# Moving the query and key projection of the last FoX pair into the stick-breaking stage

## The chip, the cores and the metric

The kernel runs on one core of a Trainium2 chip. The metric is the device time of one execution in microseconds (us). The profile is of one execution, with its engines called PE (TensorE's matmuls), PEld (its weight loads, which overlap the matmuls), DVE (VectorE), ACT (ScalarE), POOL (GpSimd) and SP (SyncE, which here only issues transfers).

## The reference, cut to what matters

One decoder layer over 2048 tokens of width 1024, in float32. The part that matters here is the token mixer: one input projection of the normed and modulated tokens `h`, and two groups of eight attention heads of 64.

```python
proj = h @ w_in[l]
q_f, k_f, v_f, q_s, k_s, v_s, f_logit = jnp.split(proj, offsets, axis=-1)
log_f = jax.nn.log_sigmoid(f_logit + b_fgate[l])
o_fox = forgetting_attention(q_f, k_f, v_f, log_f)   # softmax(q.k/8 + F[t] - F[s]), F = cumsum(log_f)
o_sb = stick_breaking_attention(q_s, k_s, v_s)       # sigmoid(z_ts) * prod_{s<j<t} (1 - sigmoid(z_tj))
mix = jnp.concatenate([head_rms_norm(o_fox), head_rms_norm(o_sb)], axis=-1)
x = x + gate_a * (mix @ w_out[l])
```

A gated MLP with a short convolution and a last norm follow.

## The kernel before

The tokens are cut into four blocks (`tb`) of 512, and each group's eight heads into four pairs (`p`) of two. A *unit* is one pair and one block: `units` lists them as stick-breaking (`sb`) pair 0, blocks 0 to 3, then pairs 1 to 3, then the same for `fox`, 32 in all. Attention is causal, so block 3 is the longest unit of a pair. A unit's attention (`attend`) makes logits on TensorE (`logits`, L378 and L379), works on them (stick-breaking: two sigmoids on ScalarE, a scan along the keys on VectorE, a product on GpSimd or VectorE; FoX: sum, minimum and exponential), and then goes through groups of two key blocks (`weighted`): four transposes (L388), a split of the result into a high and a low part by ScalarE and VectorE (L392, L393), and four matmuls with the values (L397). A pair has 72 such groups: 6, 14, 22 and 30 in its four blocks. At its end a unit stores its output (L509).

All products are of numbers split into a high and a low part, so each matrix product is three matmuls: high by high, high by low, low by high.

The projection of a unit runs ahead of its attention. `proj` loads the block of `h` as eight tiles from DRAM (L346; ten buffers), accumulates the queries (L281, 24 matmuls of 128x512) in one of two projection banks, and calls `finish_proj`. That splits the queries into `q2` (L289 on ScalarE, L290 on VectorE), spreads them over the two halves of the partitions into `Q` by four copies from SBUF to SBUF (L293), does the same with the keys (L281, 24 matmuls; L300, whose split is recorded at L44 and L45; copies into `K` at L303), and then makes the values. Values are made for two pairs at once by an even pair (L320, 96 matmuls of 128x256, spilled to DRAM for the other); an odd pair only loads them (L307). `Q` has two buffers, `K` five, `V` six, and the split tiles `q2` two. With block 0 of a pair, `load_w` loads and splits its weights (L256, L261).

`interleave` weaves the steps of the next unit's projection evenly between those of the current attention; in FoX a third generator, `late_mod`, prepares later weights, and the last unit carries the first part of the output projection (L629). The order in each engine's queue is then planned when the kernel is built, from the program's order and the buffers, and an instruction whose operands and buffers are there can be placed long before its place in the program. SP issues nearly all transfers, in order.

The pool `px` lies to the right in SBUF and holds four tiles `xt` of 4 KB per partition for the first stage's tokens. It is closed where FoX begins; the forget sums `Fb` (L672) and FoX's other tiles take its space.

Of the kernel before, what the change touches and what calls it, by code (L numbers as in the profile page):

```python
# [8 lines left out]
F32 = mybir.dt.float32  # L9
F32R = mybir.dt.float32r  # L10
# [6 lines left out]
P = 128  # L17
S = 2048
D = 1024
KT = D // P  # L20
HD = 64
NH = 8
NPAIR = 8
TB = 512
NTB = S // TB
# [8 lines left out]
def kernel(ctx: ExitStack, tc: tile.TileContext, x, c, w_ada, b_ada, g_attn, w_in, b_fgate,  # L34
                      g_out_fox, g_out_sb, w_out, g_mlp, w_up, conv_w, conv_b, w_down, g_final, out):
    nc = tc.nc
    x, out = x[0], out[0]
    w_ada, w_in, w_out, w_up, conv_w, w_down = w_ada[0], w_in[0], w_out[0], w_up[0], conv_w[0], w_down[0]

    def f(t):  # L40
        return t.bitcast(F32)

    def split(hi, lo, src, lo_engine=None):
        nc.scalar.activation(hi, src, AF.Copy)  # L44
        (lo_engine or nc.gpsimd).tensor_sub(lo, src, f(hi))  # L45

    const = ctx.enter_context(tc.tile_pool(name="const", bufs=1))
    dram = ctx.enter_context(tc.tile_pool(name="dram", bufs=1, space=DRAM))

    hs = [[dram.tile([P, 2, TB], F32, name=f"hs{t}_{k}") for k in range(KT)] for t in range(NTB)]  # L50
# [6 lines left out]
    vs = {k: [[dram.tile([P, 4, 2, P], F32, name=f"vs_{k}{p}_{t}") for t in range(NTB)] for p in range(2)]  # L57
          for k in ("sb", "fox")}
    zs = [dram.tile([4 * NH, P], F32, name=f"zs{t}") for t in range(NTB)]
    log_f = dram.tile([NTB * NH, TB], F32, name="log_f")  # L60
    fs = dram.tile([NH, S], F32, name="fs")
    rstd = [dram.tile([2 * NPAIR, TB], F32, name=f"rstd{t}") for t in range(NTB)]
# [68 lines left out]
    def interleave(main, n, fillers):  # L131
        live = [[g, k, 0] for g, k, _ in fillers if g is not None]
        for i, _ in enumerate(main):
            tick()
            for e in live:
                while e[2] < (i + 1) * e[1] / n:
                    e[2] += 1
                    if next(e[0], StopIteration) is StopIteration:
                        e[2] = 1 << 30
        for g, _, whole in fillers:  # L140
            if g is not None and whole:
                drain(g)
# [33 lines left out]
    def h_tile():  # L176
        return sl_.tile([P, 2, TB], F32R, name="hp", bufs=10)
# [101 lines left out]
    def accumulate(acc, n, w, h, kt):  # L279
        for i, (a, bb) in enumerate(((0, 0), (0, 1), (1, 0))):  # L280
            nc.tensor.matmul(acc, w[kt][:, a, n], h[:, bb], start=kt == 0 and i == 0, stop=kt == KT - 1 and i == 2)  # L281

    def finish_proj(kind, p, tb, aq, w, hts, res, ak=None):
        Q = sb.tile([P, 2, 2, TB], F32R, name="Q", bufs=2)
        K = sb.tile([P, 2, TB], F32R, name="K", bufs=5)
        V = sb.tile([P, 4, 2, P], F32R, name="V", bufs=6)
        q2 = sl_.tile([P, 2, TB], F32R, name="q2", bufs=2)
        k2 = sl_.tile([P, 2, TB], F32R, name="q2", bufs=2)
        nc.scalar.activation(q2[:, 0], aq, AF.Copy, scale=-HD ** -0.5)  # L289
        nc.vector.scalar_tensor_tensor(q2[:, 1], aq, -HD ** -0.5, f(q2[:, 0]), ALU.mult, ALU.subtract)  # L290
        for h in range(2):
            for r in range(2):
                nc.sync.dma_start(f(Q[r * HD:(r + 1) * HD, h]), f(q2[h * HD:(h + 1) * HD]))  # L293
        if ak is None:
            ak = pj()
            for kt in range(KT):
                accumulate(ak, 1, w[0], hts[kt], kt)
                if kt % 2:
                    yield
        split(k2[:, 0], k2[:, 1], ak, nc.vector)  # L300
        for h in range(2):
            for r in range(2):
                nc.sync.dma_start(f(K[r * HD:(r + 1) * HD, h]), f(k2[h * HD:(h + 1) * HD, r]))  # L303
        yield
        spill = vs[kind][p // 2][tb]
        if p % 2:
            nc.sync.dma_start(f(V), spill)  # L307
        else:
            V1 = sb.tile([P, 4, 2, P], F32R, name="V", bufs=6)
            forget = (kind, p) == ("sb", 0)  # L310
            step, width = (1, 2 * P + NH) if forget else (2, 2 * P)
            if forget:
                zn = px.tile([P, 4, NH], F32, name="zn", bufs=1)
            for i in range(0, 4, step):
                av = pj()
                for t in range(step):
                    tok = slice((i + t) * P, (i + t + 1) * P)
                    for kt in range(KT):
                        for m, (a, bb) in enumerate(((0, 0), (0, 1), (1, 0))):
                            nc.tensor.matmul(av[:, t * width:(t + 1) * width], hts[kt][:, a, tok],  # L320
                                             w[1][kt][:, bb, 0:width],
                                             start=kt == 0 and m == 0, stop=kt == KT - 1 and m == 2)
                        if kt % 4 == 3:
                            yield
                if forget:
                    nc.vector.tensor_copy(zn[:, i], av[:, 2 * P:width])
                av = av[:, 0:step * 2 * P].rearrange("p (t e h d) -> p t e h d", t=step, e=2, h=2)
                for e, v in enumerate((V, V1)):
                    v = v[:, i:i + step]
                    split(v[:, :, :, 0:HD], v[:, :, :, HD:P], av[:, :, e], nc.vector)  # L330
            if forget:
                b = pt()
                nc.tensor.transpose(b[0:4 * NH, 0:P], zn.rearrange("p t n -> p (t n)"), ident)
                zt = px.tile([4 * NH, P], F32, name="zt", bufs=1)
                nc.scalar.activation(zt, b[0:4 * NH, 0:P], AF.Identity, bias=bf_c)
                nc.sync.dma_start(zs[tb], zt)
            nc.sync.dma_start(spill, f(V1))
        res.append((Q, K, V))
        yield

    def proj(kind, p, tb, w, res):
        hts = []
        aq = pj()
        for kt in range(KT):
            h = h_tile()
            nc.sync.dma_start(f(h), hs[tb][kt])  # L346
            hts.append(h)
            accumulate(aq, 0, w[0], h, kt)
            if kt % 2:
                yield  # L350
        yield from finish_proj(kind, p, tb, aq, w, hts, res)

    def norm_proj(tb, xts, w, res):
        aq = pj()
# [170 lines left out]
    def late_mod():  # L525
# [47 lines left out]
        nc.vector.scalar_tensor_tensor(mod_m[:, 0], mod_m[:, 0], 1.0, cols[:, R_GM:R_GM + KT], ALU.add, ALU.mult)  # L573
        yield

    units = [(k, p, tb) for k in ("sb", "fox") for p in range(4) for tb in range(NTB)]
    weights = {}
    results = {}

    def proj_gen(u, xts=None):  # L580
        kind, p, tb = u
        if tb == 0:
            weights[kind, p] = load_w(kind, p)
            results[kind, p] = []
        if (kind, p) == ("sb", 0):
            return norm_proj(tb, xts or load_x(tb), weights[kind, p], results[kind, p])
        return proj(kind, p, tb, weights[kind, p], results[kind, p])
# [71 lines left out]
    for i, u in enumerate(units):  # L659
        kind, p, tb = u  # L660
        nxt = units[i + 1] if i + 1 < len(units) else None
        if u == ("sb", 1, 0):
            forget_sums()
        if u == ("fox", 0, 0):
            tick(1 << 20)
            close_pool("sx", "px")
            sx = open_pool("fx", side="right")
        if kind == "fox" and tb == 0:
            Fbs = [[sx.tile([P, TB], F32, name="Fb", bufs=8) for _ in range(NTB)] for _ in range(2)]
            for t in range(NTB):  # L670
                for h in range(2):
                    nc.sync.dma_start(Fbs[h][t],  # L672
                                      fs[2 * p + h:2 * p + h + 1, t * TB:(t + 1) * TB].to_broadcast([P, TB]))
        if kind == "fox":
            n = sum(2 * (2 + 2 * tb + j2 + 1) for j2 in range(2)) + 1
        else:
            n = sum(2 * (tb + 1 + 2 * tb + j2 + 1) for j2 in range(2)) + 1
        if i >= len(units) - 2:
            head_scale(i - len(units) + 2, pt(), sx)
        if nxt is None:  # L680
            drain(lm)
            close_pool("sl", "psa")
            psc = open_pool("psc", side="right", space=PSUM)
            p2a = open_pool("p2a")
            loaded = [load_o(0, p) for p in range(3)]
            wo = []
            tail = first_mix(loaded)
        steps = nxt and (KT + 11 if nxt[:2] == ("sb", 0) else KT - 1 if nxt[1] % 2 else KT + 4)
        interleave(attend(kind, p, tb, results[kind, p], Fbs), n,
                   [(nxt and proj_gen(nxt), steps, True),  # L690
                    (lm if kind == "fox" and (p, tb) != (0, 0) else None, 4, False), (tail, 12, True)])
    drain(first_out())
    tick(1 << 20)
# [327 lines left out]
```

## Time and profile before

| | |
|---|---|
| median of 3 runs | 3142.77 us (3141.69 to 3145.11) |
| the profiled execution | 3141.04 us, span 3139.3 us |
| TensorE matmul busy | 2967.0 us (95%) |
| TensorE weight loads busy | 2511.6 us (80%) |
| VectorE, ScalarE, GpSimd busy | 2145.5, 1691.0, 1227.1 us (68%, 54%, 39%) |
| stick-breaking attention from pair 1 on | 353.4 to 922.0 us of the span |
| FoX attention | 922.0 to 1602.1 us of the span |

The times of a stretch are counted from the start of the span. Busy time of an engine is the union of its instructions' records; since matmuls overlap in theirs, a busy TensorE need not be at its peak. The units' ends used below are the times at which SP issues the store of a unit's output.

### The profile page before, as it was taken

The page shows a single profiled execution, that of the slowest core. Times are in us where ns is not written, and L with a number is a line of the kernel's source. Part 1 is how long each engine was busy: PE and PEld are TensorE (multiplying, and loading weights), DVE is VectorE, ACT ScalarE, POOL GpSimd, SP SyncE. Part 2 cuts the span into 40 slices and gives each one's busy share as a digit, 9 for nine tenths or more (in the row PEclk, how much of TensorE's full clock was granted, in tenths as well). Part 3 has the DMA queues.
Part 4 walks back from the last instruction along what each step waited for, and adds up shares of the span by engine and source line. Part 5 has one row for each costly group of instructions (what it writes and reads, how often), then busy time and mean ns, then how long its engine had stood idle before and what let it go on. Part 6 is the DMA issues. An engine that isn't in the chain of part 4 may idle for free. (4 is left out here: it accounts for less than half of the span.)

```text
span 3139.3 us, 46425 instructions
## 1 busy us (share of the span) xinstructions
PE 2967.0 (95%) x15934; PEld 2511.6 (80%) x15934; DVE 2145.5 (68%) x3342; ACT 1691.0 (54%) x3161; POOL 1227.1 (39%) x1387
## 2 busy tenths in 40 slices
PE   6889998989989999999999999999899998999998
PEld 5778787877878889888877678888678887888887
DVE  6787888878875876556843587778987776354253
ACT  5666776666756676567744444444444444343332
POOL 1554455456553242242212344344444442322321
PEclk8999999999999999999999999999999999999999
DMA  9547542555336696585446632222222223554552
GB/s 267 177 140 255 168 136 69 182 185 155 123 108 221 214 314 211 158 313 162 164 158 222 212 97 86 86 83 83 82 82 89 85 81 130 190 199 161 189 199 90
DMA packets 292940, 496.51 MB, mean 158 GB/s; under 512 B 29448, under 2 KB 177664, under 8 KB 291680
## 3 DMA queue, kind: packets, MB, share of 16 engines
q1 hardware_dynamic: 281072, 480.92, 47.9%
q10 hardware_dynamic: 11632, 12.63, 1.1%
q8 instruction: 126, 2.06, 0.3%
q14 instruction: 110, 0.90, 0.1%
HBM read 352.61 MB, written 90.51 MB: 141 GB/s over the span
## 5 line engine op out<-in xcount | busy, mean ns | idle before, releaser
L810 PE MATMUL ps_o<-oa,wu 128*128 128x512 f32 x2088 | 503.5, 392 | 14.4 <-DVE oa L45 6.9
L810 PEld LDWEIGHTS ps_o<-oa,wu 128*128 128x128 f32 x2088 | 390.5, 188 | 105.5 <-DVE oa L45 10.7
L397 PE MATMUL ps_pv<-at,V 128*128 128x256 f32 x2304 | 410.9, 296 | 41.6 <-DVE at L393 24.8
L393 DVE TENSOR_TENSOR at<-ps_pt,at 128x512 fp32r<-128x512 f32 (+1 forms) x576 | 366.0, 653 | 102.8 <-ACT at L392 99.8
L281 PE MATMUL ps_pj<-hp,w_qk 128*128 128x512 f32 x1512 | 418.4, 406 | 11.1 <-ACT hp L44 3.1
L420 POOL TENSOR_TENSOR a<-a,r 128x512 f32<-128x512 f32 (+3 forms) x240 | 283.4, 1182 | 368.8 <-DVE r L416 112.3
L392 ACT ACTIVATE at<-ps_pt 128x512 fp32r<-128x512 f32 (+1 forms) x576 | 319.4, 577 | 179.8 <-PE ps_pt L388 147.3
L397 PEld LDWEIGHTS ps_pv<-at,V 128*128 128x128 f32 x2304 | 337.0, 192 | 84.6 <-DVE at L393 42.8
L281 PEld LDWEIGHTS ps_pj<-hp,w_qk 128*128 128x128 f32 x1512 | 275.7, 191 | 65.4 <-POOL hp L45 4.0
L45 DVE TENSOR_TENSOR wd<-wdraw,wd 128x1024 fp32r<-128x1024 f32 x88 | 112.4, 1277 | 261.4 <-ACT wd L44 261.4
L378 PE MATMUL ps_qk<-K,Q 128*128 128x512 f32 (+2 forms) x640 | 264.1, 414 | 11.3 <-DMA K<-q 5.8
L419 DVE TENSOR_TENSOR_SCAN r<-r 128x513 f32<-128x513 f32 x192 | 258.0, 1355 | 21.7 <-ACT r L410 14.5
L45 POOL TENSOR_TENSOR g<-graw,g 128x512 fp32r<-128x512 f32 x84 | 141.3, 1684 | 326.8 <-ACT g L44 326.8
L960 PE MATMUL ps_o<-wd,g 128*128 128x512 f32 x1040 | 250.8, 391 | 8.8 <-ACT g L44 8.8
L810 PE MATMUL ps_t<-ob,wu 128*128 128x512 f32 x984 | 243.2, 392 | 0.0
L320 PE MATMUL ps_pj<-w_v,hp 128*128 128x256 f32 (+1 forms) x1536 | 234.1, 291 | 4.8 <-DVE q L45 2.2
L379 PE MATMUL ps_qk<-K,Q 128*128 128x512 f32 (+2 forms) x640 | 238.1, 373 | 0.0
L960 PEld LDWEIGHTS ps_o<-wd,g 128*128 128x128 f32 x1040 | 196.2, 189 | 50.0 <-ACT g L44 9.2
L44 ACT ACTIVATE wu<-wuraw 128x512 fp32r<-128x512 f32 x214 | 133.2, 626 | 185.5 <-PE ps_o L810 111.5
L320 PEld LDWEIGHTS ps_pj<-w_v,hp 128*128 128x128 f32 x1536 | 211.8, 193 | 15.5 <-DVE q L45 3.1
L810 PEld LDWEIGHTS ps_t<-ob,wu 128*128 128x128 f32 x984 | 186.2, 189 | 39.4 <-DVE wu L45 0.3
L388 PE MATMUL ps_pt<-edge,a 128*128 128x128 f32 x1088 | 187.3, 281 | 27.6 <-POOL a L420 14.7
(217 smaller groups left out, 5743.3 us busy)
## 6 DMA issues: line engine op xcount, KB each, us to landing
hp<-hs SPq DMA_DIRECT2D x224, 512.0 KB
wuraw<-in_w_up_dram SPq DMA_DIRECT2D x84, 512.0 KB
wdraw<-in_w_down_dram SPq DMA_DIRECT2D x84, 512.0 KB
Q<-q SPq DMA_DIRECT2D x128, 256.0 KB
g<-u SPq DMA_DIRECT2D x42, 512.0 KB
graw<-g SPq DMA_DIRECT2D x84, 256.0 KB
hs<-hp SPq DMA_DIRECT2D x32, 512.0 KB
K<-q SPq DMA_DIRECT2D x128, 128.0 KB
```

The source lines that it names most:

```text
L45: (lo_engine or nc.gpsimd).tensor_sub(lo, src, f(hi))
L281: nc.tensor.matmul(acc, w[kt][:, a, n], h[:, bb], start=kt == 0 and i == 0, stop=kt == KT - 1 and i == 2)
L320: nc.tensor.matmul(av[:, t * width:(t + 1) * width], hts[kt][:, a, tok], w[1][kt][:, bb, 0:width], start=kt == 0 and m == 0, stop=kt == KT ...
L378: nc.tensor.matmul(b[:, :cw], Q[:, hl, 0, qcols], K[:, hl, :cw], start=True, stop=False)
L379: nc.tensor.matmul(b[:, :cw], Q[:, hl, 1, qcols], K[:, hl, :cw], start=False, stop=True)
L392: nc.scalar.activation(at[:, 0, lo:], b[:, lo:], AF.Copy)
L393: nc.vector.tensor_sub(at[:, 1, lo:], b[:, lo:], f(at[:, 0, lo:]))
L397: nc.tensor.matmul(o[:, 0:2 * P], V[kt // 4][:, kt % 4, hl, :], rhs, start=first and kk == 0 and w == 0, stop=last and kk == 1 and w == 1)
L419: nc.vector.tensor_tensor_scan(rev, rev, rev, 1.0, ALU.mult, ALU.bypass)
L420: (nc.vector if (ch + qi) % 4 == 0 else nc.gpsimd).tensor_mul(a[:, :need], a[:, :need], r[:, 1:need + 1])
L810: nc.tensor.matmul(b, w[:, p, j], o[:, q], start=first and i == 0, stop=last and i == 2, skip_group_check=True)
L960: nc.tensor.matmul(banks[t][n], g[:, a, t * P:(t + 1) * P], w[:, b, n * TB:(n + 1) * TB], start=k == 0 and i == 0, stop=k == NKD - 1 and i ...
```

## The change

The queries and keys of FoX pair 3 are no longer made in FoX. A new generator `far_proj(tb)` makes them for one block of tokens; it is appended to the next unit's projection in the last unit (block 3) of each stick-breaking pair, so that pair 0 makes block 0, pair 1 block 1 and so on. It accumulates queries and keys together in both projection banks over eight loads of `h`, splits them as before, and stores both split tiles in new DRAM tiles (`qks`). The first call loads and splits the weights once, and keeps them in the four buffers of `xt`. The number of filler steps of these four units grows by ten. In FoX, `stored_proj` replaces the projection of pair 3: it loads `Q` and `K` from DRAM in the same eight pieces, and the values as before, in one step.

```diff
+    qks = [[dram.tile([P, 2, TB], F32, name=f"{n}s{t}") for n in "qk"] for t in range(NTB)]
...
+    def spread_q(Q, q2):
         for h in range(2):
             for r in range(2):
-                nc.sync.dma_start(f(Q[r * HD:(r + 1) * HD, h]), f(q2[h * HD:(h + 1) * HD]))
+                nc.sync.dma_start(f(Q[r * HD:(r + 1) * HD, h]), q2[h * HD:(h + 1) * HD])
+
+    def spread_k(K, k2):
+        for h in range(2):
+            for r in range(2):
+                nc.sync.dma_start(f(K[r * HD:(r + 1) * HD, h]), k2[h * HD:(h + 1) * HD, r])
...
+    far = []
+
+    def far_proj(tb):
+
+        base = FAR * P
+        for kt in range(0 if far else KT):
+            raw = sl_.tile([P, 2, P], F32, name="raw_qk", tag="wraw", bufs=3)
+            nc.sync.dma_start(raw, w_in[kt * P:(kt + 1) * P, base:base + 5 * P].rearrange(
+                "p (a n) -> p a n", n=P)[:, 0:5:4, :])
+            if kt % 2 == 0:
+                two = px.tile([P, 2, 2, 2, P], F32R, name="w_far", tag="xt", bufs=4)
+            w = two[:, kt % 2]
+            split(w[:, 0], w[:, 1], raw)
+            far.append(w)
+        yield
+        aq, ak = pj(), pj()
+        for kt in range(KT):
+            h = h_tile()
+            nc.sync.dma_start(f(h), hs[tb][kt])
+            accumulate(aq, 0, far, h, kt)
+            accumulate(ak, 1, far, h, kt)
+            yield
+        q2 = qk_split(aq)
+        k2 = sl_.tile([P, 2, TB], F32R, name="q2", bufs=2)
+        split(k2[:, 0], k2[:, 1], ak, nc.vector)
+        for d, t in zip(qks[tb], (q2, k2)):
+            nc.sync.dma_start(d, f(t))
+        yield
+
+    def stored_proj(kind, p, tb, res):
+        Q, K, V = qkv_tiles()
+        spread_q(Q, qks[tb][0])
+        spread_k(K, qks[tb][1])
+        nc.sync.dma_start(f(V), vs[kind][p // 2][tb])
+        res.append((Q, K, V))
+        yield
...
     def proj_gen(u, xts=None):
         kind, p, tb = u
+        if (kind, p) == ("fox", FAR):
+            return stored_proj(kind, p, tb, results.setdefault((kind, p), []))
...
         steps = nxt and (KT + 11 if nxt[:2] == ("sb", 0) else KT - 1 if nxt[1] % 2 else KT + 4)
+        if nxt and nxt[:2] == ("fox", FAR):
+            steps = 1
+        ahead = nxt and proj_gen(nxt)
+        if (kind, tb) == ("sb", NTB - 1):
+            ahead, steps = chain(ahead, far_proj(p)), steps + KT + 2
         interleave(attend(kind, p, tb, results[kind, p], Fbs), n,
-                   [(nxt and proj_gen(nxt), steps, True),
+                   [(ahead, steps, True),
```

## Rows read from the trace of the kernel before

**Rows 1.** Windows by pair: length, busy (count) by engine, clock, DMA share, GB/s.
```profile
353.41:533.92 180.51, 162.75 (x1061) 142.24 (x1060) 160.45 (x220) 128.88 (x288) 94.22 (x145) 0.97 0.38 114
533.92:735.60 201.68, 188.79 (x1199) 165.87 (x1198) 162.68 (x222) 132.17 (x293) 96.66 (x153) 0.99 0.55 172
735.60:922.00 186.40, 166.06 (x1067) 144.76 (x1066) 155.18 (x200) 126.44 (x277) 110.92 (x150) 0.97 0.37 112
1278.38:1465.57 187.19, 184.62 (x1213) 166.30 (x1212) 112.33 (x285) 117.26 (x224) 66.71 (x81) 1.00 0.71 234
1465.57:1602.06 136.49, 130.40 (x847) 112.97 (x844) 104.25 (x271) 95.39 (x172) 24.06 (x43) 0.99 0.40 129
```

**Rows 2.** Windows, line L281 alone (query and key matmuls): PE busy, PEld busy.
```profile
353.41:533.92 180.51, 33.35 (x123) 21.95 (x123) 0.97 0.38 114
533.92:735.60 201.68, 67.66 (x256) 45.56 (x254) 0.99 0.55 172
735.60:922.00 186.40, 38.91 (x141) 24.95 (x141) 0.97 0.37 112
1339.94:1465.57 125.63, 50.08 (x192) 35.18 (x192) 1.00 0.79 269
...
1465.57:1602.06 136.49, 0.00 (x0) 0.00 (x0) 0.99 0.40 129
```

**Rows 3.** Window in the down-projection, columns as in the first group.
```profile
2669.00:2747.50 78.50, 78.50 (x348) 65.01 (x347) 23.69 (x18) 28.96 (x37) 31.19 (x19) 1.00 0.58 189
```

**Rows 4.** Windows: block 3 of stick-breaking pairs 0 to 3, FoX pair 2's blocks 2, 3.
```profile
250.53:353.41 102.88, 95.65 (x542) 79.86 (x541) 82.98 (x113) 68.51 (x141) 47.01 (x70) 1.00 0.71 241
462.67:533.92 71.25, 58.58 (x363) 49.16 (x362) 65.98 (x83) 49.88 (x110) 42.38 (x59) 0.95 0.28 89
653.37:735.60 82.23, 71.30 (x420) 59.61 (x419) 68.90 (x85) 53.87 (x116) 44.28 (x64) 0.98 0.46 148
850.70:922.00 71.30, 58.36 (x354) 49.23 (x353) 59.60 (x72) 45.30 (x94) 40.31 (x49) 0.95 0.28 86
1339.94:1465.57 125.63, 123.06 (x783) 109.55 (x782) 76.88 (x188) 82.36 (x149) 52.77 (x55) 1.00 0.79 269
```

**Rows 5.** Windows inside block 3 of stick-breaking pairs 1, 2 and 3.
```profile
472.00:520.00 48.00, 35.63 (x211) 28.29 (x209) 46.25 (x50) 35.26 (x75) 33.63 (x41) 0.93 0.20 54
680.00:712.00 32.00, 23.31 (x138) 18.25 (x139) 31.72 (x35) 22.62 (x46) 20.50 (x28) 0.96 0.09 20
864.00:904.00 40.00, 29.35 (x168) 23.74 (x168) 38.51 (x42) 28.33 (x57) 28.34 (x34) 0.91 0.11 34
```

**Rows 6.** The same windows, projection banks alone: PE, PEld, DVE, ACT.
```profile
472.00:520.00 48.00, 0.00 (x0) 0.00 (x0) 0.00 (x0) 0.65 (x2) 0.93 0.20 54
680.00:712.00 32.00, 0.00 (x0) 0.00 (x0) 0.66 (x1) 0.61 (x1) 0.96 0.09 20
864.00:904.00 40.00, 0.00 (x0) 0.00 (x0) 0.00 (x0) 0.00 (x0) 0.91 0.11 34
```

**Rows 7.** Timeline: start, length (us), instruction; a split, two groups of transfers.
```profile
455.94 0.69 DVE L45 TENSOR_TENSOR q<-ps_pj,q 128x512 fp32r<-128x512 f32 x1 [0.21 <-ACT q L44]
...
499.57 2.40 SPq L303 DMA_DIRECT2D K<-q  x4
...
926.04 4.83 SPq L672 DMA_DIRECT2D Fb<-fs  x8
```

**Rows 8.** Windows, line L629 in pair 3, line L320 in pair 2.
```profile
1465.57:1602.06 136.49, 24.95 (x96) 17.22 (x96) 0.99 0.40 129
...
1339.94:1465.57 125.63, 7.45 (x49) 6.52 (x47) 1.00 0.79 269
```

**Rows 9.** Groups by line and form: lines L290, L45 (count, ns minimum/median/maximum).
```profile
L290 DVE SCALAR_TENSOR_TENSOR q<-ps_pj,q x32: 660/684/693, 61.3 to 1452.2; 128x512 fp32r<-128x512 f32 x32
...
L45 DVE TENSOR_TENSOR q<-ps_pj,q x27: 664/691/693, 293.6 to 1473.5; 128x512 fp32r<-128x512 f32 x27
L45 POOL TENSOR_TENSOR w_qk<-raw_qk,w_qk x32: 727/741/1056, 730.7 to 1329.7; 128x256 fp32r<-128x256 f32 x32
```

**Rows 10.** Windows, line L281 alone, block 3 of stick-breaking pairs 0 and 1.
```profile
250.53:353.41 102.88, 53.59 (x201) 36.30 (x201) 1.00 0.71 241
462.67:533.92 71.25, 8.96 (x35) 6.30 (x36) 0.95 0.28 89
```

More of the change, by code (lines that the diff above doesn't have):

```diff
@@ L281, in accumulate, with qkv_tiles, qk_split, finish_proj @@
             nc.tensor.matmul(acc, w[kt][:, a, n], h[:, bb], start=kt == 0 and i == 0, stop=kt == KT - 1 and i == 2)
[L283 to L286, printed above, removed]
+    def qkv_tiles():
+        return (sb.tile([P, 2, 2, TB], F32R, name="Q", bufs=2), sb.tile([P, 2, TB], F32R, name="K", bufs=5),
+                sb.tile([P, 4, 2, P], F32R, name="V", bufs=6))
+    def qk_split(aq):
         q2 = sl_.tile([P, 2, TB], F32R, name="q2", bufs=2)
-        k2 = sl_.tile([P, 2, TB], F32R, name="q2", bufs=2)
         nc.scalar.activation(q2[:, 0], aq, AF.Copy, scale=-HD ** -0.5)
         nc.vector.scalar_tensor_tensor(q2[:, 1], aq, -HD ** -0.5, f(q2[:, 0]), ALU.mult, ALU.subtract)
+        return q2
+    def spread_q(Q, q2):
         for h in range(2):
             for r in range(2):
-                nc.sync.dma_start(f(Q[r * HD:(r + 1) * HD, h]), f(q2[h * HD:(h + 1) * HD]))
+                nc.sync.dma_start(f(Q[r * HD:(r + 1) * HD, h]), q2[h * HD:(h + 1) * HD])
[3 more added lines that the diff above has]
+                nc.sync.dma_start(f(K[r * HD:(r + 1) * HD, h]), k2[h * HD:(h + 1) * HD, r])
+    def finish_proj(kind, p, tb, aq, w, hts, res, ak=None):
+        Q, K, V = qkv_tiles()
+        q2 = qk_split(aq)
+        k2 = sl_.tile([P, 2, TB], F32R, name="q2", bufs=2)
+        spread_q(Q, f(q2))
         if ak is None:
@@ L300, in finish_proj @@
         split(k2[:, 0], k2[:, 1], ak, nc.vector)
-        for h in range(2):
-            for r in range(2):
-                nc.sync.dma_start(f(K[r * HD:(r + 1) * HD, h]), f(k2[h * HD:(h + 1) * HD, r]))
+        spread_k(K, f(k2))
         yield
@@ L351, in proj @@
         yield from finish_proj(kind, p, tb, aq, w, hts, res)
+    far = []
[18 more added lines that the diff above has]
+            yield
+        q2 = qk_split(aq)
+        k2 = sl_.tile([P, 2, TB], F32R, name="q2", bufs=2)
+        split(k2[:, 0], k2[:, 1], ak, nc.vector)
[3 more added lines that the diff above has]
+    def stored_proj(kind, p, tb, res):
+        Q, K, V = qkv_tiles()
+        spread_q(Q, qks[tb][0])
[3 more added lines that the diff above has]
+        yield
     def norm_proj(tb, xts, w, res):
@@ L574, in late_mod, with chain @@
         yield
+    def chain(*gens):
+        for g in gens:
+            yield from g
     units = [(k, p, tb) for k in ("sb", "fox") for p in range(4) for tb in range(NTB)]
@@ L578 @@
     results = {}
+    FAR = 3
     def proj_gen(u, xts=None):
         kind, p, tb = u
+        if (kind, p) == ("fox", FAR):
+            return stored_proj(kind, p, tb, results.setdefault((kind, p), []))
         if tb == 0:
```

## Prediction

> **What bounds the kernel now.** I read four views in this order. The busy time of each stretch comes first, cut at the ends of pairs: stick-breaking pairs 1 to 3 and FoX pairs 2 and 3 [rows 1, 2]. TensorE is busy for 81% to 99% of every one, so the page alone says "TensorE bound" everywhere. But matmuls overlap in their records, so busy is not full: the counts have to be priced.
>
> The price comes from a stretch of the down-projection in which TensorE does nothing but 128x512 matmuls without a gap: 78.50 us for 348, so 0.2256 us each [rows 3]. A block's queries and keys take 2 x 8 x 3 = 48 such matmuls, 10.83 us, and the four blocks of the last FoX pair 43.3 us.
>
> Where do those 192 matmuls stand? The stretch from 1339.94 to 1465.57 (attention of FoX pair 2, blocks 2 and 3) holds exactly 192 of the projection's matmuls [rows 2], and pair 3's own stretch holds none. So the planned order runs ahead of the program, and the work that the change takes away lies wholly in those 125.63 us. There TensorE is busy 123.06 us, VectorE 76.88 and ScalarE 82.36 [rows 4]: this stretch is TensorE's.
>
> The third view is the last block of each stick-breaking pair (four units) [rows 4]. TensorE's idle there is 7.2, 12.7, 10.9 and 12.9 us, 43.8 in all. The fourth cuts three of these units finer: for 48, 32 and 40 us in a row no projection matmul runs at all, VectorE is busy 96% to 99%, and TensorE 73% to 74% at a granted clock of 0.91 to 0.96 [rows 5, 6]. Why is there no filler? The next pair's projections have run up against their buffers: the keys of block 1 of pair 2 are split at 455.94 and are copied to their five-buffer tile only at 499.57, 43 us later [rows 7]. The new work needs none of those buffers. These holes are VectorE's time, and what TensorE does in them besides may be cheap.
>
> **The change, part by part.** *Removed from FoX.* 192 matmuls go, 43.3 us at the dense price: that is the most that the stretch can lose, and leaves 82.3 us. How fast can attention go with nothing else in TensorE's queue? Pair 3's stretch shows that: 136.49 us for its 72 weighted-sum steps (groups of two key blocks), among them 96 output-projection matmuls of the same shape [rows 1, 8], 21.7 us. So (136.49 - 21.7) / 72 = 1.594 us a step. Blocks 2 and 3 have 22 + 30 = 52 steps, 82.9 us; 49 value matmuls of half the width remain [rows 8], at half the price 5.5 us (an estimate). Together 88.4, so a gain of 37.2 us. If the output projection hid under pair 3's other work, the pace is 136.49 / 72 = 1.896, 98.6 us, and the gain 27.0. I take 37, between 27 and 43. VectorE keeps 71 us of work there and ScalarE under 82, so neither takes over below 88. The splits of four blocks go too; they were not the bound there.
>
> *Added to stick-breaking.* The same 48 matmuls for each of four blocks, plus per block two ScalarE copies and two VectorE splits of 0.684 and 0.691 us (median), 1.375 together [rows 9]. From below: matmuls in a hole cost nothing where VectorE sets the pace, but VectorE's own 1.375 us counts in full; four blocks, 5.5 us. From above: the pairs themselves, which differ mainly in how many projection matmuls they carry. Pair 2 has 133 more than pair 1 and takes 21.2 us longer, 0.71 of the 30.0 us at the dense price; against pair 3 it has 115 more and takes 15.3 longer, 0.59 of 25.9 [rows 1, 2]. At 0.71 a block costs 7.6 us, four 30.7. The last unit of pair 0 against that of pair 1 is worse still: 166 more matmuls, 31.6 us longer, 0.845 of 37.4 [rows 4, 10]; at that price four blocks cost 36.6.
>
> These slopes mix in other work (weight splits on VectorE in pair 0's unit, different values), and they are paid mostly where TensorE is already full. The new work has the hole beside it: 120 us of holes at about a quarter idle, some 32 us by the busy rows, for three blocks of 32.5 us. So I take 3.6 us for pairs 1 to 3, nearer to the hole than to the slope, and for pair 0, whose last unit already carries 201 such matmuls, the mean slope of 0.65, 7.0 us. Sum 17.8, call it 18; ends 5.5 and 36.6.
>
> *Room by another count.* Matmul records give 43.8 us of idle for 43.3 us of work, a tight fit, by which I would take the slope of 0.71 and forecast about 3137. The weight loads of the same rows leave 23.0, 22.1, 22.6 and 22.1 us uncovered, 89.8 in all [rows 4], by which the work fits twice and the price lies nearer the hole's. [...]
>
> *Weights.* The eight raw loads and splits move from FoX to the end of pair 0. GpSimd's eight splits take 8 x 0.741 = 5.9 us [rows 9]; in that unit it is busy 47 of 103 us [rows 4], so they hide, and they come well before a use. If that cover is gone, 5.9 us once. The split weights sit in the four old x tiles, which are idle by then: nothing.
>
> *Transfers.* Each block brings eight 512 KB loads and two 512 KB stores on SP's queue; the FoX side loses the eight loads, and reads its queries and keys in the same eight copies, now from DRAM. Transfers share 9% to 20% in the holes [rows 5], so bandwidth is free. A store waits for the split, and behind it in SP's queue stand the next projection's loads; who waits for them is the next pair's projection, which is 43 us ahead of its buffer [rows 7]. Nothing, or a few us if that lead is used up. The two small query/key buffers and both projection banks are held a block longer, against the same lead.
>
> *Start of FoX.* The tiles of the forget sums take over space in which the new weights lay. They are loaded at 926.04 [rows 7], 4 us after the last stick-breaking block is stored, and the last hole ends at 904, so the fourth block should be done. If it is late, FoX starts late by as much.
>
> *Sum.* The profiled execution took 3141.04 us, 1.7 below the median of the runs. 3141.0 - 37 + 18 = 3122; on the median 3123.8. I predict **3124 us**; by the nearer ends of both terms, 3111 to 3135.
>
> **The rivals.** *Slower.* The planned order puts filler matmuls ahead of attention's transposes and logits in TensorE's queue, which runs in order, and VectorE, which must not wait in the holes, waits. Place: the four last units; price 0.845 of dense, 36.6 us. With FoX giving 27, the result is 3152. It decides once stick-breaking costs more than FoX gives: at 37, that is 0.85 of 43.3. For it: the unit of pair 0. Against it: in pairs 1 to 3 the slope is 0.59 to 0.71 even without holes singled out.
>
> *No change.* TensorE's work is the same in total, and if its queue is the bound everywhere, moving is worth nothing: 30.7 back for 27 to 37 gained, 3137 to 3147. For it: busy shares of 81% and more. Against it: 120 us with no filler at a reduced clock.
>
> *Almost all of it.* The holes take the work at VectorE's 5.5 us and FoX falls to TensorE's bare remainder, 43: 3105. For it: the weight-load rows. Against it: FoX's pace without filler, and pair 0, which has no hole.
>
> **How the numbers follow.** Forecast 0.56, almost all of it 0.15, no change 0.12, slower 0.17. A change of 0.2%, 6.3 us, is about what a measurement of this kernel can tell from none. So faster 0.71, same 0.12, slower 0.17. The range of 3105 to 3147 holds the forecast, the no-change case, half of the larger gain and the mild end of the slower one.
>
> **What would show it.** FoX pair 2's blocks 2 and 3, 125.63 us now, should fall to 82 to 99 with no 128x512 projection matmul for pair 3 in them; pair 3's stretch should stay near 136 us. In stick-breaking the holes should carry 48 matmuls each with VectorE still over 90% busy; pairs 1 to 3 should grow by about 4 us each, and pair 0's last unit by 7. The prediction is wrong if VectorE's busy share in the holes falls below about 85%, if the next pair's projections come late to attention, or if FoX stays at its length because VectorE or ScalarE, not TensorE, holds it.

## The result, and the profile after

The changed kernel took 3148.38 us (median of 10 runs, 3143.89 to 3152.46), the kernel before 3141.19 beside it (10 runs): a ratio of 1.0022 [1.0012, 1.0032]. The forecast was 3124, its range ended at 3147. Timed once more, in another session (below), the change came out at 1.0001 [0.9992, 1.0010]. So it is worth nothing, or costs about 0.2%. (The ratios here and below come with their 95% intervals; they are taken over all the runs and differ by up to 0.0008 from the quotients of the medians.) The profiled execution took 3144.33 us (span 3142.5), against 3141.04 (3139.3) before.

The times at which SP issues the stores of the units' outputs say where the time went (us of the span; differences are of the unrounded times; the first unit's end, which no edit touches, varies by 2 us between runs). The last column is the fastest version found, told below as e14; it has a second edit besides, the square on ScalarE.

| end of | before | after | | blocks 2 and 3 alone | |
|---|---|---|---|---|---|
| stick-breaking pair 0, block 3 | 353.4 | 362.5 | +9.1 | 352.5 | -0.9 |
| pair 1, block 0 | 367.5 | 383.5 | +16.1 | 367.6 | +0.2 |
| pair 1, block 3 | 533.9 | 555.9 | +22.0 | 533.7 | -0.2 |
| pair 2, block 3 | 735.6 | 758.6 | +23.0 | 739.1 | +3.5 |
| pair 3, block 3 | 922.0 | 950.6 | +28.6 | 931.5 | +9.5 |
| FoX pair 2, block 1 | 1339.9 | 1368.3 | +28.4 | 1349.9 | +9.9 |
| FoX pair 2, block 3 | 1465.6 | 1468.2 | +2.6 | 1461.3 | -4.3 |
| FoX pair 3, block 3 | 1602.1 | 1601.8 | -0.2 | 1594.9 | -7.2 |
| the kernel | 3139.3 | 3142.5 | +3.3 | 3137.5 | -1.8 |

Stick-breaking pays 28.6 us and FoX gives back 28.8. What is left, 3.5 us, stands after attention, in the output projection and the MLP, which no edit touches. From attention's end to the last instruction the profiled execution of before took 1537.2 us, that of after 1540.7. A second profile of after took 1543.9 there, and the version in the last column 1542.6. This part scatters from execution to execution, and so do the stages before it. Four later runs (e1, e7, e12 and e13, told below) have the change's stick-breaking, and their edits, where they have one, touch FoX alone. With the profile above that makes five, in which stick-breaking ends 26.1 to 33.7 us later than before. In two runs with the stick-breaking of before (e2 and e8) it ends at 922.4 and 917.0. So a difference of under about 5 us between two single profiles decides nothing. Steadier in the five is where the growth stands: pair 0 ends 7.9 to 11.7 us later, pair 1 takes 12.6 to 13.1 us more, pair 2 changes by -0.9 to 1.0, and pair 3 takes 4.7 to 11.7 more.

The windows of the changed kernel that answer to [rows 1, 4] (length, then busy time and count of PE, PEld, DVE, ACT, POOL, the granted clock, DMA share, GB/s): three pairs, the four last units, then the two FoX stretches.

```profile
362.50:555.90 193.40, 176.43 (x1136) 154.00 (x1135) 171.64 (x230) 135.64 (x301) 105.08 (x150) 0.98 0.43 136
555.90:758.60 202.70, 195.78 (x1229) 173.63 (x1228) 161.39 (x223) 131.61 (x291) 89.42 (x148) 0.98 0.59 190
758.60:950.60 192.00, 174.76 (x1134) 152.69 (x1133) 160.62 (x204) 128.48 (x283) 111.63 (x155) 1.00 0.47 144
256.35:362.50 106.15, 100.33 (x558) 85.36 (x557) 74.84 (x106) 64.50 (x134) 41.97 (x64) 0.98 0.82 276
480.40:555.90 75.50, 61.91 (x388) 52.07 (x387) 69.87 (x85) 51.56 (x111) 45.61 (x61) 0.95 0.27 88
675.90:758.60 82.70, 78.20 (x450) 67.26 (x449) 68.19 (x86) 53.65 (x115) 37.08 (x59) 0.96 0.54 180
875.50:950.60 75.10, 61.01 (x399) 51.94 (x399) 63.56 (x76) 46.59 (x97) 44.05 (x52) 1.00 0.26 83
1368.30:1468.20 99.90, 86.06 (x608) 77.66 (x606) 78.55 (x184) 78.52 (x143) 52.50 (x56) 0.93 0.55 173
1468.20:1601.80 133.60, 128.10 (x845) 111.36 (x843) 104.35 (x270) 95.46 (x172) 24.07 (x44) 1.00 0.39 128
```

The pairs grew by 12.9, 1.0 and 5.6 us. Pair 2's last unit, 82.23 before, is 82.70 now with TensorE busy 78.20 instead of 71.30: there the idle time was used. Pair 1's and pair 3's last units grew by 4.3 and 3.8 us, and TensorE still idles 13.6 and 14.1 us in them, more than before (12.7 and 12.9 [rows 4]). FoX's stretch fell from 125.63 us to 99.90, and TensorE, which was idle 2.6 us in it, is now idle 13.8.

Where did the moved matmuls go? The next fence is of windows of the changed kernel, the tile of the new weights alone (PE, PEld, ACT, POOL): one window for each block's 48.

```profile
273.80:291.40 17.60, 12.24 (x48) 8.50 (x48) 0.00 (x0) 0.00 (x0) 1.00 0.92 280
420.50:442.30 21.80, 12.80 (x48) 8.58 (x48) 0.00 (x0) 0.00 (x0) 1.00 0.90 333
659.10:677.30 18.20, 11.97 (x48) 8.52 (x47) 0.00 (x0) 0.00 (x0) 1.00 0.93 298
819.90:841.10 21.20, 12.96 (x48) 8.54 (x48) 0.00 (x0) 0.00 (x0) 1.00 0.93 346
```

None stands in a hole (a stretch in which no projection matmul runs). Block 1's run ends at 442, block 3's at 841, while the last units that were to carry them begin at 480 and 875. The holes are still there, later. Windows of before and then of after, the projection banks alone (PE, PEld, DVE, ACT), each just inside the longest stretch of its pair in which no projection matmul starts:

```profile
468.80:520.90 52.10, 0.00 (x0) 0.00 (x0) 1.04 (x3) 1.08 (x3) 0.93 0.25 74
674.70:713.40 38.70, 0.00 (x0) 0.09 (x1) 0.66 (x1) 0.61 (x1) 0.96 0.21 62
856.80:909.20 52.40, 0.00 (x0) 0.00 (x0) 1.14 (x3) 1.09 (x3) 0.93 0.31 98
```

```profile
490.60:542.90 52.30, 0.00 (x0) 0.00 (x0) 1.03 (x3) 0.87 (x3) 0.93 0.28 85
718.70:738.30 19.60, 0.00 (x0) 0.06 (x1) 0.68 (x1) 0.59 (x1) 0.83 0.34 106
892.90:937.70 44.80, 0.00 (x0) 0.00 (x0) 1.14 (x3) 1.04 (x3) 1.00 0.36 114
```

Pair 1's hole is as long as it was, pair 3's lost 7.6 us, and only pair 2's was halved. The new matmuls went ahead of the holes, into stretches that were already full, and only in pair 2 did they push much of other work into one. The next fence has windows of before around the places where blocks 1, 2 and 3 went: TensorE is busy for 114.29 of their 115 us, at a granted clock of 1.00. Block 2's place was as full as the others'.

```profile
410.00:450.00 40.00, 40.00 (x270) 36.30 (x269) 32.18 (x45) 28.09 (x58) 20.54 (x35) 1.00 0.27 94
640.00:675.00 35.00, 35.00 (x208) 30.54 (x207) 22.17 (x32) 18.80 (x41) 12.26 (x21) 1.00 0.79 255
800.00:840.00 40.00, 39.29 (x266) 35.27 (x265) 34.01 (x45) 29.56 (x63) 21.50 (x32) 1.00 0.22 73
```

In FoX the stretch has a new bound. Windows of 20 us of the changed kernel, columns as in the first fence:

```profile
1368.30:1388.30 20.00, 18.68 (x140) 17.12 (x138) 12.99 (x35) 15.01 (x29) 13.21 (x13) 1.00 0.75 258
1388.30:1408.30 20.00, 8.19 (x43) 5.58 (x42) 14.97 (x19) 17.01 (x30) 18.68 (x17) 0.77 0.94 300
1408.30:1428.30 20.00, 19.96 (x137) 18.64 (x136) 16.87 (x43) 15.87 (x29) 14.85 (x15) 0.89 0.02 9
```

In the second of them TensorE works 8.19 of 20 us, GpSimd 18.68 and ScalarE 17.01. The timeline of the changed kernel there (start, length, instruction, count, idle before and releaser) shows GpSimd, VectorE and TensorE:

```profile
1398.38 8.60 POOL L602 TENSOR_TENSOR hp<-hp 128x512 f32<-128x512 f32 x7
...
1399.02 7.98 DVE L540 SCALAR_TENSOR_TENSOR ls<-ls 128x4 f32<-128x4 f32 x1 [3.67 <-ACT p L502]
1406.92 1.28 DVE L443 TENSOR_TENSOR at<-ps_pt,at 128x512 fp32r<-128x512 f32 x2
...
1407.66 1.76 PE L438 MATMUL ps_pt<-edge,p 128*128 128x128 f32 x7 [11.19 <-DVE at L443]
```

GpSimd makes additions of `late_mod` (L602: sums of weight rows that ScalarE has scaled at L601). VectorE's square of a 128x4 tile (L540, median 0.165 us) begins in the middle of seven of them and ends with them, 7.98 us later. TensorE waits 11.19 us. `late_mod`'s work is not new (28 such additions in the stretch, before and after), but it stands closer: between 1376 and 1420, 25 of these additions instead of 13. The next fence has L602 alone in after, then the same line, there L552, in before.

```profile
1376.00:1420.00 44.00, 30.28 (x25) 0.84 0.67 221
```

```profile
1376.00:1420.00 44.00, 16.25 (x13) 1.00 0.91 313
```

### The profile page after: what moved, and what is told of

It is laid out like the page before. It is cut to its first block, busy times and chain, and to the rows that moved or that the text cites. A ratio compares the mean times of both kernels' runs of the same rounds, so it can differ in the third digit from the quotient of the medians.

```text
span 3142.5 us, 46429 instructions
## 1 busy us (share of the span) xinstructions
PE 2968.5 (94%) x15934; PEld 2521.2 (80%) x15934; DVE 2160.1 (69%) x3342; ACT 1689.1 (54%) x3161; POOL 1226.8 (39%) x1387
## 5 line engine op out<-in xcount | busy, mean ns | idle before, releaser
L282 PE MATMUL ps_pj<-hp,w_qk 128*128 128x512 f32 x1320 | 367.6, 409 | 10.7 <-DMA hp<-hs 4.0
L45 DVE TENSOR_TENSOR wd<-wdraw,wd 128x1024 fp32r<-128x1024 f32 x88 | 113.4, 1290 | 260.6 <-ACT wd L44 260.6
L282 PEld LDWEIGHTS ps_pj<-hp,w_qk 128*128 128x128 f32 x1320 | 243.5, 193 | 58.7 <-DMA hp<-hs 5.1
L45 POOL TENSOR_TENSOR g<-graw,g 128x512 fp32r<-128x512 f32 x84 | 141.3, 1683 | 326.9 <-ACT g L44 326.9
L460 ACT ACTIVATE r<-ps_qk 128x512 f32<-128x512 f32 (+2 forms) x320 | 173.2, 541 | 69.7 <-PE ps_qk L429 63.3
```

## The experiments

Two questions: why do four blocks cost stick-breaking 28.6 us, and what holds FoX's stretch at 100? Two theories for the second: the wait of the square, or the burst of `late_mod` as such.

**The square on ScalarE (e1), and the same edit in the kernel before (e2).**

```diff
-                    nc.vector.scalar_tensor_tensor(l, l, EPS, l, ALU.mult, ALU.mult)
+                    nc.scalar.activation(l, l, AF.Square, scale=EPS ** 0.5)
```

> The changed kernel, with the square of FoX's sums (two small operands, both in SBUF) made by ScalarE and no longer by VectorE. In the changed kernel one such square lasts 7.98 us while GpSimd runs seven additions of 128x512 back to back, and TensorE is idle for 11.2 us right behind it. Theory (VectorE waits for GpSimd at their common way into SBUF): the wait goes, attention of FoX pair 2 blocks 2 and 3 takes 88 to 92 us and not 99.9, and the time falls by 8 to 11 us, to about 3138. Rival (the stretch is as long as its other work makes it, the wait only shows where slack lies): 98 to 100 us, and 3146 to 3149.

> Control: the kernel before with the same square on ScalarE. Before, no such square lasted over 1.3 us, so by both theories the time stays within 0.1% of before, 3138 to 3144.

Measured: e1 3143.30 us against 3148.31, 0.9992 [0.9983, 1.0002]; e2 3143.61, 0.9989 [0.9978, 1.0001]. No square of e1 is long any more, and its FoX stretch is 98.1 us instead of 99.9. Windows of e1, the whole stretch and 20 us of it, columns as above:

```profile
1366.80:1464.90 98.10, 89.54 (x610) 77.94 (x609) 70.48 (x179) 78.76 (x148) 52.68 (x56) 0.97 0.58 179
...
1387.10:1407.10 20.00, 15.53 (x82) 12.33 (x82) 11.74 (x30) 18.39 (x34) 20.00 (x19) 0.83 0.97 318
```

The rival's 98 to 100 us came out. With the wait gone GpSimd is busy 20.00 of 20 us and ScalarE 18.39: the wait fell into time that was lost anyway. Between e1 and e2, both with the edit, the change is worth nothing.

**The burst spread (e7), and the control (e8).** e1 and e2 with seven steps of `late_mod` in a unit instead of four, so that it ends before FoX pair 2's block 2.

```diff
-                    (lm if kind == "fox" and (p, tb) != (0, 0) else None, 4, False), (tail, 12, True)])
+                    (lm if kind == "fox" and (p, tb) != (0, 0) else None, 7, False), (tail, 12, True)])
```

> The changed kernel with the square on ScalarE and with seven steps of the late modulation's sums in each FoX unit, not four: they then end before FoX pair 2's block 2, where in the changed kernel 28 ScalarE scalings and as many GpSimd additions fall into 40 us. Theory (this burst fills ScalarE and GpSimd, and attention waits behind it in their queues): blocks 2 and 3 of FoX pair 2 take 85 to 91 us and not 98.0 as with the square alone, pairs 0 and 1 grow by 0 to 4, and the time is 0.15% to 0.35% below before. Rival (FoX's attention has this pace anyway): 96 to 100 us, or the saving comes back in pair 1, and the time is within 0.1% of before.

> Control: the kernel before with both of these edits. By both theories blocks 2 and 3 of FoX pair 2 stay at 121 to 127 us, since 192 projection matmuls fill TensorE there, and the time is within 0.1% of before.

Measured: 3157.52 us against 3145.76, 1.0035 [1.0021, 1.0049], and 3161.16, 1.0047 [1.0032, 1.0062]. The window of e7's FoX pair 2, blocks 2 and 3:

```profile
1395.80:1480.00 84.20, 82.83 (x609) 76.00 (x607) 70.98 (x184) 62.99 (x120) 12.18 (x25) 1.00 0.65 211
```

84.2 us, TensorE busy 98%, with none of the 28 additions left in it: so `late_mod`'s burst was the bound. Its additions on GpSimd, its scalings on ScalarE and its loads went out together, and in e1's 20 us above all three are near full (DMA share 0.97). The loads weren't what held attention: others took their place (17.8 MB in e7's stretch, 17.6 in e1's), and 20 us of e7 with the DMA engines full have TensorE busy for 19.72:

```profile
1415.80:1435.80 20.00, 19.72 (x144) 17.88 (x142) 19.08 (x51) 16.43 (x28) 2.61 (x6) 1.00 1.00 390
```

Between ScalarE and GpSimd no run decides. The longest waits in e1's 20 us, 3.1 us of TensorE and 3.6 of VectorE, were for attention's own copies on ScalarE, which points to ScalarE's queue. But both kernels are slower, and both forecasts of their time missed. In e7 the last unit of FoX pair 0 takes 76.6 us, 14.3 more than before, and the units of pair 1 together 7.7 more; in e8, whose stretch kept its length (126.0), attention ends at 1616.4. The sums cost more where they went than they did in the stretch.

**A block held back to the hole (e3).** The new matmuls wait, through two small VectorE operations on the weights, for an output of the first head of the unit that carries them.

```diff
         yield
+        for n in range(2):
+            c_ = far[0][0:HD, 0, n, 0:1]
+            nc.vector.scalar_tensor_tensor(c_, gate[-1], 0.0, f(c_), ALU.mult, ALU.add)
         aq, ak = pj(), pj()
...
+                if (kind, tb, j2, hl) == ("sb", NTB - 1, 0, 0):
+                    gate.append(oT[0:HD, 0:1])
```

> The changed kernel, with each block's matmuls in stick-breaking held until the first head of that last unit is done, by a dependence of one column of the weights on that head's output (times zero). Theory (the planned order pulls the blocks of pairs 1 and 3 ahead into stretches where TensorE is full, and leaves the stretches without filler empty): the matmuls move into 496 to 536 and 896 to 928, pairs 1 and 3 give back 3 to 6 us each, stick-breaking grows by 16 to 22 us over before and not by 28.6, and the time falls by 6 to 12 us. Rival (a filler matmul costs about two thirds of its dense price wherever it stands): growth stays at 26 to 30 us and the time at 3146 to 3150.

Measured: 3162.79 us, 1.0053 [1.0033, 1.0073], where a fall of 6 to 12 us had been expected. The holes became 70, 32 and 63 us long, longer in pairs 1 and 3 than in the change (53 and 46), and stick-breaking still ended at 951.1. The held matmuls of blocks 1 and 3 did move, to 491 and 894, but each hole now ends where they begin. The next pair's projection takes the same two banks after the held block, so it stands behind it (this is read from the code, no run singles it out): in FoX attention is 18 to 49 us later than before. Holding the block back in this way doesn't use the hole.

**One block alone: block 2 (e4) and block 0 (e11).** The others are projected in FoX as before.

```diff
-        if (kind, tb) == ("sb", NTB - 1):
+        if (kind, tb) == ("sb", NTB - 1) and p in (2,):
```

> The changed kernel, with only block 2 made in stick-breaking (at the end of pair 2, weights loaded there too); blocks 0, 1 and 3 as before, with their own weights. Theory (block 2 costs under 1.5 us because it ends in a stretch without filler, and the weights cost a few): stick-breaking grows by 1 to 6 us, FoX falls by 8 to 11, the time is 3133 to 3139. Rival (two thirds of the dense price for every block, 7 us, and the weights beside it): stick-breaking grows by 10 to 13, and the time is 3140 to 3146.

> The changed kernel with only block 0 made in stick-breaking, at the end of pair 0; blocks 1 to 3 as before in FoX. Theory (pair 0's end pays in full): pair 1's block 0 ends 13 to 17 us later than before (367.5), and pairs 1 to 3 add less than 3. Rival (0.66): 6 to 9 us later there.

Measured: e4 3151.19 us against 3148.31, 1.0008 [0.9998, 1.0017]; e11 3148.46 in one run, against 3146.78. Block 2 alone costs stick-breaking 3.9 us (925.9), and the hole shrinks from 39.3 to 20.2 us. FoX gave nothing back for it, where 8 to 11 us had been expected: attention ended 6.6 us late, with a square that waited 5.21 us in the stretch. With block 0 alone pair 1's block 0 ends 15.8 us late, as expected, and stick-breaking 10.6 us late (932.6), about the dense price of 10.8; FoX gives back 7.4. Pair 0's last unit in e11 and the unit behind it, columns as above:

```profile
253.60:362.30 108.70, 102.04 (x558) 86.78 (x557) 75.39 (x107) 64.67 (x133) 41.95 (x65) 0.97 0.79 266
362.30:383.20 20.90, 19.20 (x113) 15.71 (x112) 19.69 (x35) 17.65 (x46) 8.18 (x17) 1.00 0.92 277
```

108.7 and 20.9 us where before it was 102.88 and 14.1, TensorE busy for 94% and 92%. FoX pair 2's blocks 2 and 3, first in e4 and then in e11, with 144 projection matmuls left in both:

```profile
1347.90:1475.10 127.20, 118.38 (x737) 106.00 (x737) 79.82 (x188) 80.91 (x147) 52.29 (x55) 0.95 0.72 237
```

```profile
1353.70:1470.60 116.90, 114.49 (x740) 100.52 (x739) 76.98 (x189) 80.59 (x146) 52.97 (x56) 1.00 0.75 249
```

**Most of the matmuls left out (e5), and the weights alone (e6).** e5 leaves out 144 of the 192 moved matmuls, so its queries and keys of FoX pair 3 are not the reference's; e6 only loads and splits the weights in stick-breaking, and projects in FoX as before.

```diff
-            accumulate(aq, 0, far, h, kt)
-            accumulate(ak, 1, far, h, kt)
+            if kt in (0, KT - 1):
+                accumulate(aq, 0, far, h, kt)
+                accumulate(ak, 1, far, h, kt)
```

> The changed kernel, with 144 of the 192 moved matmuls left out (six of each block's eight row tiles of the weights are not multiplied); loads, weights, splits, stores and waits for buffers stay. So queries and keys of the last FoX pair are not the reference's. Theory (stick-breaking pays for TensorE's time, about 0.66 of the dense price): stick-breaking until 922.0 before, 950.6 in the changed kernel, ends at 927 to 933. Rival (it pays for the buffers, the transfers and the splits): 943 to 951.

> The kernel before, with the eight loads and splits of the last FoX pair's weights added at the end of stick-breaking pair 0, as the changed kernel has them, and nothing made from them. Theory (the planner pulls them into the unit before, where ScalarE, GpSimd and SP's queue then hold up the third block's tiles): stick-breaking pair 0 ends 4 to 7 us later than before (353.4), and the rest follows. Rival (hidden, as predicted): 0 to 2 us later.

Measured, one run each against 3145.76: 3124.52 and 3145.67 us. e5's stick-breaking ends at 928.7, inside its theory's range and 6.7 us after that of before and 21.9 before that of after: 144 matmuls, 32.5 us at the dense price, cost 21.9 us, 0.67 (0.60 to 0.83 against the other four profiles with the change's stick-breaking). e6 ends stick-breaking at 921.8 and attention at 1603.4, and pair 0 not 4 to 7 us late but 4.8 early: the weights cost nothing that one profile can show. The price is mainly the matmuls', not the transfers', stores, splits or buffers.

**Other places (e9, e10, e14), with the change itself again (e12) and e1 again (e13).** With the square on ScalarE in e9, e10, e13 and e14. e9 moves blocks 1 to 3; e10 moves all four, block 0 beside block 2 at the end of pair 2; e14 moves blocks 2 and 3.

```diff
-        if (kind, tb) == ("sb", NTB - 1):
+        if (kind, tb) == ("sb", NTB - 1) and p in (2, 3):
...
-        if (kind, p) == ("fox", FAR):
+        if (kind, p) == ("fox", FAR) and tb in (2, 3):
```

> The changed kernel with the square on ScalarE, and with block 0 of the last FoX pair projected in FoX as before (with weights of its own); blocks 1 to 3 in stick-breaking, weights at the end of pair 1. In the changed kernel stick-breaking is 16.1 us late when pair 1's block 0 ends (1.5 times the 10.8 us of block 0's matmuls), and the three pairs after it add 12.6 (0.39 of 32.5 us). Theory (only the end of pair 0 pays in full, since TensorE is full there; FoX pair 2 is held at 98 us by other engines, so that 10.8 us of matmuls put back there cost little): stick-breaking ends 11 to 17 us later than before, FoX pair 2's blocks 2 and 3 take 98 to 105, attention ends at 1587 to 1596, time 0.15% to 0.4% below before. Rival (0.66 of the dense price wherever the block stands, on both sides): stick-breaking ends 20 to 23 us later, the two blocks take 104 to 108, attention ends at 1599 to 1603, time within 0.1% of before.

> The changed kernel with the square on ScalarE, and with block 0 made at the end of stick-breaking pair 2, beside block 2, not at the end of pair 0. Theory (pair 2's end is the cheap place): stick-breaking ends 13 to 20 us later than before, FoX pair 2's blocks 2 and 3 take 97 to 100, attention ends at 1586 to 1593, time 0.2% to 0.4% below before. Rival (0.66 of the dense price wherever): 27 to 30 us later, attention ends at 1599 to 1602, time within 0.1% of before.

> The change itself, timed beside the next two on one chip. Theory (the change costs stick-breaking what it saves FoX, and the few microseconds by which it came out slower lie after attention, where the times of every kernel scatter): attention ends at 1600 to 1603 us again, ratio to the kernel before 0.999 to 1.002, within 0.002 of the next run. Rival (the 7.98 us wait of the square costs about 9 us in the end, as the two ratios 1.0022 and 0.9992 from two chips say): 1.002 again, and 0.003 above the next run.

> The change with the square on ScalarE once more, on the same chip as the change itself. Theory: within 0.002 of the change, attention ends at 1599 to 1602 us. Rival: 0.003 below the change.

> Square on ScalarE; only blocks 2 and 3 are made in stick-breaking, blocks 0 and 1 in FoX as before. Theory (the dear blocks are those of pairs 0 and 1, and FoX's bursts make the last moved blocks worth little): stick-breaking ends 9 to 15 us later than before (930 to 937), FoX pair 2's blocks 2 and 3 take 105 to 116 us, attention ends 1592 to 1602 us, ratio 0.997 to 1.000. Rival (a flat 0.66 of the dense price on both sides): stick-breaking 14.3 later, FoX 14.3 shorter, attention's end at 1602, ratio 1.000.

| | median, before beside it | ratio | stick-breaking | FoX | attention's end |
|---|---|---|---|---|---|
| e9, blocks 1 to 3 | 3140.84, 3146.78 | 0.9984 [0.9974, 0.9995] | +21.6 | -28.0 | -6.4 |
| e10, block 0 in pair 2 | 3142.26, 3146.78 | 0.9987 [0.9978, 0.9996] | +25.8 | -32.1 | -6.3 |
| e12, the change | 3144.92, 3145.25 | 1.0001 [0.9992, 1.0010] | +33.3 | -31.2 | +2.1 |
| e13, square on ScalarE | 3143.48, 3145.25 | 0.9995 [0.9984, 1.0006] | +26.1 | -30.5 | -4.4 |
| e14, blocks 2 and 3 | 3137.86, 3145.25 | 0.9970 [0.9960, 0.9979] | +9.5 | -16.6 | -7.2 |

(The last three columns are differences to the profile of before, in us.) e12 and e13 lie 0.0006 apart, and e12's square waited about 8 us again, so the wait has no price that these runs can tell. e9's stick-breaking grew as its rival said, while its FoX stretch (102.4 us) and its time came out as the theory said; e10 fell between its two forecasts; attention's end missed its forecast by 1 us in e12 and e13; e14 met its theory in every figure. Half of the change, e14, is 0.30% faster than before (0.23% by the medians). The square alone had given 0.11% [0.22% to nothing] in e2, on another chip, so the blocks' own part is some 0.1% to 0.2%, not much more than the two intervals allow. e14 and e13, both with the square on ScalarE and timed side by side, also lie 0.2% apart. Windows of e14: pairs 2 and 3, then FoX pair 2's blocks 2 and 3 with 96 projection matmuls left in them.

```profile
533.70:739.10 205.40, 197.52 (x1244) 174.73 (x1243) 163.88 (x223) 135.21 (x301) 101.69 (x160) 0.99 0.63 201
739.10:931.50 192.40, 174.83 (x1118) 152.28 (x1118) 160.67 (x203) 127.74 (x281) 113.29 (x152) 0.98 0.43 135
1349.90:1461.30 111.40, 107.63 (x709) 95.56 (x707) 73.60 (x185) 82.07 (x152) 53.14 (x57) 0.98 0.73 238
```

The same FoX stretch of e9, with 48 left:

```profile
1359.20:1461.60 102.40, 96.94 (x658) 86.06 (x657) 71.78 (x180) 79.91 (x150) 52.50 (x56) 0.98 0.69 218
```

Pair 2 grew by 3.7 us, pair 3 by 6.0. The FoX stretch lost 14.2 of the 25.7 us that it loses in the full change, and TensorE is still busy for 97% of it. The third block takes another 9.0 us off (e9), the fourth 3 to 6 (99.1 us in e13, 98.1 in e1, 96.8 in e10): only of the last block does the burst keep most.

## Why the prediction was wrong

**The step that failed most is the price in stick-breaking:** "So I take 3.6 us for pairs 1 to 3, nearer to the hole than to the slope", with 7.0 for pair 0, 18 in all. It was 28.6. The single blocks measure 10.6 (block 0, e11), about 12 (block 1: e9's 21.6 less e14's 9.5), 3.5 to 3.9 (block 2, e14 and e4) and 6.0 (block 3, e14), each from single profiles with the scatter told above. Together they are 32 us, within the 26.1 to 33.7 of the five. The pairs were to grow by about 4 us each and grew by 12.9, 1.0 and 5.6. Only block 2 costs what was forecast or less. The reason is that "the new work has the hole beside it" was taken from the place of the step in the program. The prediction had itself read from [rows 2] that the plan runs projections far ahead of the program, and from [rows 7] that it does so as long as buffers allow. It said that the new work needs none of the buffers that held the next pair back, and so it could run ahead too. The trace shows that it did, to 420 to 442 and 820 to 841, long before the holes; that the free buffers let it is read from the code. Without a hole the price is that of full stretches: e5 measured 0.67 of the dense price over the four blocks, inside the slopes of 0.59 to 0.71 that the prediction had worked out and set aside (28.6 of 43.3 is 0.66). The rival "no change", 3137 to 3147 with 30.7 given back, had this number almost right. The forecast of 37 - 18, a gain of 19 us, became 28.8 - 28.6, or 0.2.

**Room by weight loads was no room.** The 89.8 us that the loads leave uncovered spoke for the lower price. But by [rows 3] the loads cover only 65.01 of 78.50 us, 83%, where TensorE is full. At that share (an estimate, since attention's matmuls are of other shapes) the four units have 40 us to spare, no more than the 43.8 by matmul records. And room by either count is of no use to work that is not placed in it.

**The gain in FoX was 28.8 instead of 37.** The stretch fell to 99.9, just outside the named 82 to 99. "Neither takes over below 88" failed: it compared ScalarE's 82 and VectorE's 71 us with the length of the whole stretch. `late_mod` comes in bursts that fill ScalarE and GpSimd for 20 us on end (e1: 18.39 and 20.00 of 20), while TensorE and VectorE wait; GpSimd, with 52.77 us in [rows 4], was not weighed at all. The pace itself was right: without the burst the same work took 84.2 us (e7), against 88.4 worked out and 82.9 for the steps alone. So two blocks gain 16.6 us of their 21.7 (e14), three 28.0 of 32.5 (e9), and four 28.8 to 32.1 of 43.3 (the change, e1, e10, e12 and e13).

**What held.** No projection matmul for pair 3 is left in FoX, its pair 3 took 133.6 us against "near 136", the weights are hidden (e6), and FoX did not start late for want of a tile (its pair 0 ends 26.6 us late, stick-breaking 28.6). VectorE stayed over 90% busy in the holes (50.08 of 52.30 us in pair 1's), because little came into them. Two readings were off without weight in the sum: in [rows 1] TensorE's lowest share is 89%, not 81% (82% is that of last units in [rows 4]), and the nearer end of 27 us gives 3134, not 3135.

**What stays open.** Why block 0 costs about its full dense price in pair 0, where TensorE is busy for 94% and not 100%, and block 1 even more in pair 1 (12.6 to 13.1 us for 10.8), wasn't taken apart. In the changed kernel a split of keys on ScalarE waits 6.1 us at 352.6 for copies out of the two-buffer tile `q2`; the total of such waits is 16.9 us in both kernels, so it is no proof. Nor is it shown why block 2 alone gained nothing in FoX (e4). Its stretch has as many projection matmuls left as e11's and is 10.3 us longer; TensorE is idle for 8.8 us of it instead of 2.4, at a mean granted clock of 0.95 instead of 1.00, and the longest of its waits, 5.2 us, is behind the square. One profile each doesn't show whether that would come again.

## What to carry to other kernels

Where a planner may run work ahead, a free slot is filled only by work that cannot start before it: look at what holds the present filler back, and if it doesn't hold the new work, price that by the full stretches ahead of the slot. Before work is taken off an engine that bounds a stretch, cut the stretch into short windows and look for bursts of the others, since shares over the whole of it don't show them. When a move is a wash in sum, price its parts singly: here moving two of the four blocks gained some 0.1% to 0.2%, and moving all four nothing.

## What the runs showed of the hardware

A VectorE operation with both inputs in SBUF, a square of 128x4 whose median is 0.165 us, lasted 7.98 us beside seven GpSimd additions of 128x512 that ran without a gap for 8.60 us; it ended with the last of them (1407.00 against 1406.98). A square lasted 7.99 us in the second profile of the change, 7.73 in e5 and 5.21 in e4, and each of these ended with the last of such additions, too. But a run of additions doesn't always keep VectorE out: in before the longest square in this stretch took 1.25 us (1415.28 to 1416.52) and ended with one addition (1416.50), while further ones ran on without a gap to 1421.48. What decides between the two isn't shown. On ScalarE no square took over 0.22 us (e1, e9, e14). The Trainium skill (SBUF — State Buffer, SBUF: two separate sides) says that VectorE, in an operation with two inputs in SBUF, and GpSimd, in one that reads SBUF, share a pair of ports under an exclusive lock: the one that starts first keeps it for its whole instruction, and the other waits. The trace of before agrees, with a wait for one instruction; in the changed kernel VectorE was shut out for a run of seven.
